# Seven block products in place of eight for the input product of a hybrid encoder layer, with its results passed through DRAM

## The chip, the cores and the metric

The kernel runs on one NeuronCore of a Trainium2 chip, in one launch. The metric is the time of the launch on the device, in microseconds (us). The engines are named as in the profile: PE (TensorE, with PEld for its weight loads), DVE (VectorE), ACT (ScalarE), POOL (GpSimd) and SP (SyncE, which here only issues DMAs).

## The reference

One encoder layer for 1024 positions of width 1024, in float32. The input is normalised and multiplied by one wide matrix; three branches use slices of the result, each branch's output goes through its own matrix and a gate, the sum through an output matrix, and a gated feed-forward block follows.

```python
h = rmsnorm(x, g[0])
proj = h @ w_in[l]
(mq, mk, mv, mo, mi, mf, dq, dk, dv, rq, rk, rv, rg, gates) = split_in(proj)
qk = jax.nn.silu(causal_dwconv(jnp.concatenate([mq, mk], axis=-1), mlstm_conv[l]))
hm = mlstm(mq_c, mk_c, mv, mi + bias_i, mf + bias_f)        # 4 heads of 256, scan over chunks
hm = jax.nn.sigmoid(mo) * head_rms(hm)
hd = diff_attention(dq, dk, dv, lam)                        # 8 heads, two softmaxes each
hr = jax.nn.silu(rg) * head_rms(retention(rq, rk, rv))      # 4 heads of 256, scan over chunks
y = (gm * (hm @ w_mlstm_out) + gd * (hd @ w_diff_out) + gr * (hr @ w_ret_out)) @ w_out
x = x + rmsnorm(y, g[1])
f = (silu(a) * u) @ w_ffn_out                               # a, u = split(rmsnorm(x) @ w_ffn_in)
x = x + rmsnorm(f, g[3])
```

The input matrix has 14344 columns: 112 blocks of 128, and eight columns for the mLSTM's input and forget gates.

## The kernel before, in words

Every large product is made of float32 operands that are split in two parts, a rounded high part and a low part (`split_sbuf`, L95 to L97: ACT casts, DVE subtracts), and of three matmuls per pair of operands (`mm3`, L99 to L104: high by high, high by low, low by high). All matmuls of these products carry the lines 102 to 104; the tiles tell the products apart.

The normalised input is turned to lie with its features on the partitions (`transposed`, L230) and held as `hh` and `hl` for the whole first half of the kernel. The input product runs in blocks. A `proj_block` (L192) makes 128 columns of the result for all positions: the weights are the stationary operand, 512 positions stream, eight steps along the features, two halves. A `nat_block` (L199) makes 256 columns of v with the positions on the partitions: 128 positions are stationary and 256 columns stream. A block's two halves are two passes of 24 matmuls, each cut into two steps, so a step is 12 matmuls of 512 columns; a step of a `nat_block` is 24 matmuls of 256.

What a block makes stays in SBUF in large tiles (tag `T`, 33 of 4 KB per partition) until its core has used it; only the gates go to DRAM. The mLSTM's q and k pass through a convolution of four taps (`conv_evac`, L342): one DVE multiplication and three multiply-adds, then Silu on ACT.

`stream` (L159) turns the list of blocks into a sequence of dense steps, with weights loaded two blocks and split one block ahead. Three cores run one after another: `mlstm_core` (L480), `diff_core` (L611) and `ret_core` (L745). Each is a generator that states how much of its work has passed, and `weave` (at the end of `trunk`) puts dense steps between its parts: 2.0 steps per unit of the two scans, 184 steps for the 832 units of the differential core. A scan has 32 chunks of 128 positions (4 heads by 8), two units each. The differential core has 64 turns, a head and a block of 128 queries each; the blocks of a head go from the longest (1024 keys) to the shortest (128 keys). In a turn the attention weights of one block are transposed, the scores of the next are made (PE L631, DVE L633 adds the bias and takes the maximum, ACT L638 takes the exponential, DVE L647 joins the two softmaxes), and the values of the first are multiplied (L668). Within these bounds a scheduler orders the instructions of each engine when the kernel is built, the earlier ones in the program first where they are ready.

Behind the cores come the branch products (`merge_blocks`, L823: 16 passes of two steps per branch, the gate's sigmoid and the sum of the branches on ACT and DVE), the output product (`out_blocks`) and the feed-forward block. The two products of the feed-forward block already use a scheme of seven products on a two by two grid of blocks: seven left operands (A11, A12, A22 and the sums S1 to S4, class `Seven`) by seven right ones (B11, B21, B22 and T1 to T4, class `Up`, L1025), 84 matmuls per pair of column blocks where the plain product has 96. Its start (`feed_forward`, L1129) works on two units while the left sums are made.

Of the kernel before, what the change touches and what calls it, by code (L numbers as in the profile page):

```python
# [36 lines left out]
N_T, N_WS, N_WH, N_WL, N_D, N_H = 33, 2, 4, 4, 4, 11  # L37
# [3 lines left out]
def trunk(ctx: ExitStack, tc: tile.TileContext, x, norm_gains, w_in, mlstm_conv, mlstm_gate_bias,  # L41
# [42 lines left out]
    g_dram = [dram.tile([D, S], F32, name=f"gate{i}") for i in range(3)]  # L84
    x2_dram = dram.tile([S, D], F32, name="x2_dram")
# [5 lines left out]
    def half_tile(shape=(P, HALF), dtype=F32):  # L91
        return small(list(shape), "s2k", dtype, bufs=N_H)
# [36 lines left out]
    class Block:  # L129
        def __init__(self, specs, run, own=False, pre=None):  # L130
            self.specs, self.run, self.own, self.pre = specs, run, own, pre
            self.stage = self.w = None

        def load(self):
            if self.stage is None:
                self.stage = []
                for src, shape in self.specs:
                    t = big(shape, F32, "ws") if self.own else pool.tile(shape, F32, tag="ws", bufs=N_WS, name=nm("ws"))
                    for a, part in src if isinstance(src, list) else [(src, t)]:
                        nc.sync.dma_start(part if part is t else t[:, :, part], a)  # L140
                    self.stage.append(t)
                if self.pre is not None:
                    self.pre()

        def split(self):
            self.load()
            if self.w is None:
                self.w = []
                for t, (_, shape) in zip(self.stage, self.specs):
                    if self.own:  # L150
                        hi, lo = big(shape, F32R, "wh"), big(shape, F32R, "wl")
                    else:
                        hi = pool.tile(shape, F32R, tag="wh", bufs=N_WH, name=nm("wh"))
                        lo = pool.tile(shape, F32R, tag="wl", bufs=N_WL, name=nm("wl"))
                    split_sbuf(hi, lo, t)
                    self.w.append((hi, lo))
# [26 lines left out]
    def proj_half(act, w, sh, evac):  # L183
        ps = psum(True)
        for kt in range(KT):
            mm3(ps, (w[0][:, kt, :], w[1][:, kt, :]), act.slot(sh, kt), kt == 0, kt == KT - 1)
# [4 lines left out]

    def proj_block(act, w_src, c, evac, order=(0, 1), **kw):  # L192

        def run(w):
            for sh in order:
                yield from proj_half(act, w[0], sh, evac)
        return Block([cols_of(w_src, c)], run, **kw)

    def nat_block(act, c, evac):  # L199

        def run(w):
            for st in range(NT):
                ps = psum(True)
                for kt in range(KT):
                    wh, wl = w[kt // 4]
                    mm3(ps[:, :256], act.tile(kt, st), (wh[:, kt % 4, :], wl[:, kt % 4, :]), kt == 0, kt == KT - 1)
                evac(ps[:, :256], st)
                yield
        return Block([cols_of(w_in, c, 256, k0, 4) for k0 in (0, 4)], run)
# [20 lines left out]
    def transposed(act, src, sh, g, wide=False):  # L230


        for kt in range(KT):
            ps = psum(wide and kt % 2 == 1)
            for i in range(4):
                nc.tensor.transpose(ps[:, i * P:(i + 1) * P], src[i][:, kt * P:(kt + 1) * P], ident)
            h, l = act.slot(sh, kt)
            nc.scalar.activation(h, ps, AF.Copy, scale=pcol[:, g + kt:g + kt + 1])
            yield nc.vector.scalar_tensor_tensor(l, ps, pcol[:, g + kt:g + kt + 1], h.bitcast(F32), op0=ALU.mult, op1=ALU.subtract)  # L239

    hT = Act("h")
# [9 lines left out]

    def gate_rows():
# [5 lines left out]
        lam_in = small([P, 4, 64], "s2k", bufs=N_H)  # L258
        nc.scalar.dma_start(lam_in, diff_lambda.broadcast_to([P, 4, 64]))
        lam_pr = small([P, 2, 64], "s2k", bufs=N_H)  # L260
# [34 lines left out]
        rows = big([P, S], name="rows")  # L295
        nc.vector.memset(rows, 0.0)
# [3 lines left out]
        reset = big([MH, S], name="reset")  # L300
# [650 lines left out]

# [506 lines left out]
```

## Time and profile before

| | us |
|---|---|
| median of 3 runs (lowest to highest) | 2686.84 (2686.42 to 2688.12) |
| the profiled execution, its own time | 2687.46 |
| its span in the profile | 2685.7 |
| PE busy / DVE / ACT / POOL | 2624.1 / 1403.5 / 1089.1 / 161.7 |
| mean granted clock of PE, share of full speed | 0.991 |

In the span mLSTM's chunks run from about 120 to 564 us, the differential core from 563 to 1258 us, the retention from 1260 to 1701 us; after that the rest of the branch products, the output product from about 1900 us, the feed-forward block from 2008 us with its down product from 2460 us. A row of a group gives line, engine, operation, tiles, count, busy time and mean duration; a row of a window gives the busy time of PE, PEld, DVE, ACT and POOL with the number of instructions in brackets, then PE's granted clock, the share of the DMA engines and GB/s. Matmuls of neighbours overlap in the profile, so distances between starts, or a window that PE fills, tell more than durations.

### The profile page before, as it was taken

How to read it: one execution, taken by the hardware profiler on the slowest of the kernel's cores; microseconds unless marked ns; L12 is line 12 of the kernel's file. 1: busy time of each engine (PE TensorE's matmuls, PEld its weight loads, DVE VectorE, ACT ScalarE, POOL GpSimd, SP SyncE). 2: the span in 40 equal slices, each digit the busy share in tenths (PEclk: the TensorE clock that was granted, in tenths of full speed). 3: DMA queues.
4: the chain of work that ended last, by engine and by line, in shares of the span. 5: the costliest groups of instructions: out<-in, count | busy, mean ns of one | idle time of the engine just before them, and what ended most of it. 6: DMA issues, size and time to landing. Idle time of an engine off the chain costs nothing.

```text
span 2685.7 us, 35232 instructions
## 1 busy us (share of the span) xinstructions
PE 2624.1 (98%) x13653; PEld 2212.7 (82%) x13653; DVE 1403.5 (52%) x2953; ACT 1089.1 (41%) x2119; POOL 161.7 (6%) x209
## 2 busy tenths in 40 slices
PE   7999999999999999999999999999989999998998
PEld 6889989888888888888889897888867888886886
DVE  5465564545554555544333335445477555555857
ACT  5644443334444444445333344422344333333444
POOL 0000000000000000000000000000020101110000
PEclk9999999999999999999999999999999999998999
DMA  4111112322222222211111234722431323338343
GB/s 146 48 56 56 56 56 64 95 75 81 54 79 60 75 79 60 79 40 52 47 44 37 63 102 134 226 88 71 157 133 63 102 87 106 106 104 297 113 124 107
DMA packets 244419, 243.08 MB, mean 91 GB/s; under 512 B 11838, under 2 KB 184335, under 8 KB 244251
## 3 DMA queue, kind: packets, MB, share of 16 engines
q1 hardware_dynamic: 242816, 238.63, 28.8%
q10 hardware_dynamic: 1434, 2.20, 0.3%
q8 instruction: 107, 1.75, 0.3%
q14 instruction: 62, 0.50, 0.1%
HBM read 178.62 MB, written 53.77 MB: 87 GB/s over the span
## 4 chain that ended last, share of the span: by engine, by line
PE 78%; issue 14%; DVE 3%; DMA 2%; POOL 1%; ACT 1%; SPq 0%; ACTq 0%; DVEq 0%; POOLq 0%
PE ps L103 23%; PE ps L104 23%; PE ps L102 23%; PE ps L631 2%; PE ps L668 2%; PE ps L657 1%; PE ps L461 1%; DVE wl L97 1%; DMA hid_S<-s2k 1%; PE ps L469 1%; POOL xr L216 0%; PE ps L429 0%; DMA s2k<-branch 0%; PE ps L686 0%; POOL s2k L1125 0%
## 5 line engine op out<-in xcount | busy, mean ns | idle before, releaser
L102 PE MATMUL ps<-hh,wh 128*128 128x512 f32 x1408 | 572.3, 406 | 1.9 <-DVE hl L239 1.9
L103 PE MATMUL ps<-hl,wh 128*128 128x512 f32 x1408 | 557.6, 396 | 0.0
L104 PE MATMUL ps<-hh,wl 128*128 128x512 f32 x1408 | 557.5, 396 | 0.0
L96 ACT CAST wh<-ws 128x1024 fp32r<-128x1024 f32 (+1 forms) x197 | 196.1, 999 | 431.1 <-PE ps L103 366.7
L97 DVE TENSOR_TENSOR wl<-ws,wh 128x1024 fp32r<-128x1024 f32 (+2 forms) x197 | 227.6, 1158 | 243.6 <-ACT wh L96 238.9
L104 PEld LDWEIGHTS ps<-hh,wl 128*128 128x128 f32 x1408 | 265.0, 188 | 63.1
L102 PEld LDWEIGHTS ps<-hh,wh 128*128 128x128 f32 x1408 | 265.8, 189 | 55.7 <-DVE hl L239 2.3
L103 PEld LDWEIGHTS ps<-hl,wh 128*128 128x128 f32 x1408 | 265.7, 189 | 53.5
L102 PE MATMUL ps<-wh,hh 128*128 128x256 f32 (+1 forms) x768 | 220.1, 287 | 0.0
L103 PE MATMUL ps<-wl,hh 128*128 128x256 f32 (+1 forms) x768 | 216.3, 282 | 0.0
L104 PE MATMUL ps<-wh,hl 128*128 128x256 f32 (+1 forms) x768 | 216.1, 281 | 0.0
L102 PE MATMUL ps<-bh,wh 128*128 128x512 f32 x384 | 153.0, 398 | 1.5 <-ACT bh L96 1.5
L103 PE MATMUL ps<-bl,wh 128*128 128x512 f32 x384 | 151.7, 396 | 0.3 <-DVE bl L97 0.3
L104 PE MATMUL ps<-bh,wl 128*128 128x512 f32 x384 | 151.6, 395 | 0.0
L102 PEld LDWEIGHTS ps<-wh,hh 128*128 128x128 f32 x768 | 145.0, 189 | 0.2
L103 PEld LDWEIGHTS ps<-wl,hh 128*128 128x128 f32 x768 | 145.0, 189 | 0.2
L104 PEld LDWEIGHTS ps<-wh,hl 128*128 128x128 f32 x768 | 144.9, 189 | 0.0
L102 PE MATMUL ps<-wh 128*128 128x512 f32 x308 | 120.4, 393 | 10.7 <-ACT wh L96 10.7
L103 PE MATMUL ps<-wl,wh 128*128 128x512 f32 x308 | 121.2, 393 | 1.8 <-DVE xv L215 1.1
L104 PE MATMUL ps<-wh,wl 128*128 128x512 f32 x308 | 120.8, 392 | 0.0
L638 ACT ACTIVATE sb<-sb,nmx 128x896 f32<-128x896 f32 (+7 forms) x128 | 98.6, 771 | 50.3 <-DVE nmx L637 49.7
L96 ACT CAST wh<-s2k 128x512 fp32r<-128x512 f32 x77 | 47.7, 620 | 113.1 <-PE ps L104 103.4
(300 smaller groups left out, 4994.1 us busy)
## 6 DMA issues: line engine op xcount, KB each, us to landing
ws<-in_w_in_dram SPq DMA_DIRECT2D x110, 512.0 KB, 4.1
ws<-in_w_ffn_in_dram SPq DMA_DIRECT2D x44, 512.0 KB, 3.9
gate<-s2k SPq DMA_DIRECT2D x48, 256.0 KB, 2.0
gl<-gate SPq DMA_DIRECT2D x24, 512.0 KB, 6.2
s2k<-branch SPq DMA_DIRECT2D x48, 256.0 KB, 5.9
hid_S<-s2k SPq DMA_DIRECT2D x44, 256.0 KB, 2.9
wd<-in_w_ffn_out_dram SPq DMA_DIRECT2D x22, 512.0 KB, 7.3
s2k<-hid_S SPq DMA_DIRECT2D x44, 256.0 KB, 2.6
```

The lines of the kernel that those rows point to most:

```text
L96: nc.scalar.copy(hi, src)
L97: nc.vector.tensor_sub(lo, src, hi.bitcast(F32))
L102: nc.tensor.matmul(ps, lh, rh, start=start, stop=False, skip_group_check=more)
L103: nc.tensor.matmul(ps, lh, rl, start=False, stop=False, skip_group_check=more)
L104: nc.tensor.matmul(ps, ll, rh, start=False, stop=stop, skip_group_check=more)
L461: nc.tensor.matmul(ps[:, :P], k_t[c // 4][:, j, half_cols(c)], q_t[c // 4][:, j, half_cols(c)], start=j == 0, stop=j == 1)
L469: nc.tensor.transpose(ps[:, j * P:(j + 1) * P], hn[:, j * P:(j + 1) * P], ident)
L631: nc.tensor.matmul(ps[:, :b - a], d["q", qb // 4][:, c, half_cols(qb)], d["k", n][i][:, c, :b - a], start=i == 0, stop=i == 1)
L638: nc.scalar.activation(sb[c], sb[c], AF.Exp, bias=nmx, scale=slope, accum_out=sm[:, c:c + 1])
L657: nc.tensor.transpose(ps[:, i * P:(i + 1) * P], u["sb"][0][:, kb * P:(kb + 1) * P], ident)
L668: nc.tensor.matmul(o_ps[:, :P], u["at"][kb // 4][:, half_cols(kb)], v[kb // 4][:, kb % 4, vc], start=kb == 0, stop=kb == qb)
```

## The change

All 112 column blocks of the input product are paired into 56 units, and each unit is made by seven products of 12 matmuls (class `Unit`, shared with the feed-forward block). The rows of the left operand are the two halves of the positions, its columns the two halves of the features; the sums S1 to S4 are made once (`left_sums`), the four differences of weights for each unit on DVE (on POOL for the three units at either start). The eight gate columns get products of their own (`gate_products`). v is made like everything else with its features on the partitions and is turned where it is needed.

Nothing a unit makes stays in SBUF: q, k, gate and v of the two scans go to `m_dram` and `r_dram`, q and k of the differential core in two parts to `qk_dram`, its v, turned, to `dv_dram`, the gates with their sigmoid applied to `g_dram`. A scan loads a chunk's eight rows of 128 positions one chunk ahead (`chunk_of`), the differential core loads a head's tiles while the head before runs (`diff_load`).

The order changes: mLSTM, then retention, both with 2.6 dense steps per unit; then the rest of the input product alone; then the differential core with 64 dense steps, which are now the products of the mLSTM and the retention branch; then the third branch. The sum over the branches passes through `y_dram`, the additions on POOL. The numbers of tiles change with it.

```diff
-N_T, N_WS, N_WH, N_WL, N_D, N_H = 33, 2, 4, 4, 4, 11
+N_T, N_WS, N_W, N_D, N_H = 32, 4, 5, 4, 14
...
+    y_dram = dram.tile([D, S], F32, name="y_dram")
+    m_dram = dram.tile([MH, P, 8, S], F32, name="m_dram")
+    r_dram = dram.tile([MH, P, 8, S], F32, name="r_dram")
+    qk_dram = dram.tile([DH, 2, 2, P, S], F32, name="qk_dram")
+    dv_dram = dram.tile([S, D], F32, name="dv_dram")
...
+        for role, dst, op, x, y in (("S1", "A22", ALU.add, "A21", "A22"), ("S2", "A22", ALU.subtract, "A22", "A11"),
+                                    ("S3", "A21", ALU.subtract, "A11", "A21"), ("S4", "A12", ALU.subtract, "A12", "A22")):
+            for i in range(2):
+                nc.vector.tensor_tensor(xs[dst, i], xs[x, i], xs[y, i], op=op)
+            for i in range(2):
...
+            (b11, b21), (b12, b22) = ((t[:, LO, :], t[:, HI, :]) for t in self.raw)
+            sub = {"T1": (b12, b12, b11), "T2": (b12, b22, b12), "T3": (b11, b12, b11), "T4": (b12, b21, b12)}
+            for r in roles:
+                if r in sub:
+                    src = sub[r][0]
+                    self.eng.tensor_tensor(*sub[r], op=ALU.subtract)
+                else:
+                    src = {"B11": b11, "B21": b21, "B22": b22}[r]
+                self.w[r] = parts_tile([P, 4, P])
+                split_sbuf(*self.w[r], src)
+        def product(self, ps, right, left, more):
+            wh, wl = self.w.pop(right)
+            for q in range(4):
+                mm3(ps, (wh[:, q, :], wl[:, q, :]), self.seven.slot(left, q), q == 0 and not more, q == 3, more)
...
+        def p6(self):
+            self.product(self.x, "T2", "S2", True)
+            self.b = self.kept(self.x)
...
+    def follow(u, after):
+        u.p1()
+        u.split("T3")
+        yield
+        u.p2()
+        u.split("B22")
+        yield
+        if after is not None:
+            after.load(0)
+            after.load(1)
+        u.p6()
+        u.split("T4")
+        yield
+        u.p5()
+        if after is not None:
+            after.split("B11")
+        yield
+        u.p7()
+        if after is not None:
+            after.split("B21")
+        yield
+        u.p3()
+        if after is not None:
+            after.split("T1")
+        yield
+        u.p4()
+        if after is not None:
+            after.split("T2")
+        yield
...
+        a, b, c = units
+        for u in units:
+            u.eng = nc.gpsimd
+        a.p1()
+        a.p2(False)
+        b.load(0)
+        b.load(1)
+        b.split("B11", "B21")
+        for _ in range(3):
...
+        sums = left_sums(seven, xs)
+        for u in units:
+            u.split("T1")
+        next(sums)
+        for u in units:
+            u.p5(False)
+            u.split("T2")
...
+        def evac(j, sh, ps, part):
+            if part is None:
+                part = half_tile()
+                nc.scalar.activation(part, ps, func or AF.Copy)
+            else:
+                nc.vector.tensor_add(part, ps, part)
+                if func is not None:
+                    nc.scalar.activation(part, part, func)
+            nc.sync.dma_start(dst(j)[:, halfs(sh)], part)
...
+            for i, t in enumerate((h, l)):
+                nc.sync.dma_start(qk_dram[hd, 1 - j, i][:, halfs(sh)], t.bitcast(F32))
...
+            for role, k in terms:
+                for q in range(4):
+                    w = wif[:, (k + q) * 16:(k + q) * 16 + P]
+                    for i, part in enumerate(hT.slot(role, q)):
+                        nc.tensor.matmul(ps, w, part, start=k == 0 and q == 0 and i == 0, stop=k > 0 and q == 3 and i == 1)
...
+    def chunk_of(src, u):
+        t = u["ch"] = big([P, 8, P], name="ch")
+        c = u["c"]
+        nc.sync.dma_start(t, src[u["hd"]][:, :, c * P:(c + 1) * P])
...
+    def natural_v(ch, ones):
+        ps = natural(ch, 6)
...
+        nc.sync.dma_start(spill[hd * HD:(hd + 1) * HD, c * P:(c + 1) * P].rearrange("(j p) s -> p j s", p=P), t)
...
+    def diff_load(hd, sh, d):
+        d["q", sh] = big([P, 2, HALF], F32R, "dq")
+        d["k", sh] = [big([P, 2, HALF], F32R, "dk") for _ in range(2)]
+        for i in range(2):
+            q, k = (qk_dram[hd, j, i][:, halfs(sh)].rearrange("(c p) s -> p c s", c=2) for j in range(2))
+            for a in range(2):
+                nc.sync.dma_start(d["k", sh][i][64 * a:64 * a + 64].bitcast(F32), k)
+            nc.sync.dma_start(d["q", sh][64 * i:64 * i + 64].bitcast(F32), q)
...
+        def half(o, sh, w):
+            rows = slice(o * P, (o + 1) * P)
+            g, y = half_tile(), None
+            nc.sync.dma_start(g, g_dram[b][rows, halfs(sh)])
+            if n > 0:
+                y = half_tile()
+                nc.sync.dma_start(y, y_dram[rows, halfs(sh)])
+            def evac(ps, sh):
+                nc.vector.tensor_mul(g, ps, g)
+                if n > 0:
+                    nc.gpsimd.tensor_tensor(g, g, y, op=ALU.add)
+                if n < 2:
+                    nc.sync.dma_start(y_dram[rows, halfs(sh)], g)
                 else:
-                    nc.vector.tensor_add(y[o][:, cs], y[o][:, cs], t[:, cs])
-                if b == 2:
                     h, l = yT.slot(sh, o)
...
+    hT, hx = Seven(), {}
+    def of(cols, evac, own=False):
+        return Unit(hT, w_in, cols, evac, own)
...
+        q, k, o, v = head(m_dram, (C_MQ, C_MK, C_MO, C_MV),
+                          (lambda dst, hd: convolved(dst, 2 * hd), lambda dst, hd: convolved(dst, 8 + 2 * hd),
+                           lambda dst, hd: stored(dst, AF.Sigmoid), lambda dst, hd: stored(dst)), hd)
+        units += [v, o, q, k]
...
+    for b in BRANCHES:
+        for o in range(0, KT, 2):
+            c = C_G + b * D + o * P
+            units.append(of((c, c + P), stored(lambda j, b=b, o=o: g_dram[b][(o + j) * P:(o + j + 1) * P, :], AF.Sigmoid)))
+    ups = [up(i, own=i == 2) for i in range(FB)]
+    units[2].own = True
...
+    def projections():
+        n = 7 * (len(units) - 3)
+        side = load_branch(BRANCHES[0], 0)
+        for i, _ in enumerate(steady(units[3:])):
+            made[0] = 3 + (i + 1) // 7
+            if i >= n - 4:
+                next(side, None)
+            if i == n - 3:
+                merges[0].load()
+            if i == n - 1:
+                for r in ROLES:
+                    hT.drop(r)
+                merges[0].split()
+            yield
...
+    def everything():
+        yield from projections()
+        yield from stream(merges + more)
...
+    begin(units[:3], hT, hx, turned(hn[4:], 1, 72, hT, hx))
...
-    weave(mlstm_core(), 2.0)
-    weave(diff_core(), 184 / 832)
-    weave(ret_core(), 2.0)
+    weave(mlstm_core(), 2.6)
+    weave(ret_core(), 2.6)
+    need(len(units))
+    weave(diff_core(), 64 / 832)
     for _ in dense:
         pass
-    feed_forward(ups, turns)
+    begin(ups[:3], h2, h2x, turns)
```

The bodies not shown: `turned` makes the high part, the plain float32 copy and the low part of three of the four quarters of the input (one ACT and two DVE operations per block); `convolved` is the convolution of before on tiles of half the width; `steady` runs `follow` over the units; `begin` goes on through all seven products, unit by unit for each; `keep_hidden` and the down product are as before but for the tiles of split weights, now of 512 columns each.

## Rows read from the trace of the kernel before

**Rows 1.** The page, part 1: busy time, share and instructions of each engine.

```profile
PE 2624.1 (98%) x13653; PEld 2212.7 (82%) x13653; DVE 1403.5 (52%) x2953; ACT 1089.1 (41%) x2119; POOL 161.7 (6%) x209
```

**Rows 2.** Windows of the span; stretch, length, each engine busy, clock, DMA, GB/s.

```profile
0.00:21.00 21.00, 7.34 (x34) 6.08 (x35) 8.52 (x19) 12.98 (x21) 2.51 (x9) 0.91 0.86 285
120.00:560.00 440.00, 438.73 (x2601) 385.47 (x2600) 243.36 (x645) 188.39 (x395) 20.03 (x31) 1.00 0.22 62
570.00:1250.00 680.00, 678.02 (x3812) 579.26 (x3811) 346.55 (x1005) 292.79 (x680) 33.97 (x62) 1.00 0.24 65
1260.00:1700.00 440.00, 437.56 (x2504) 379.12 (x2503) 174.11 (x368) 169.76 (x357) 17.53 (x32) 1.00 0.26 78
2000.00:2020.00 20.00, 11.29 (x48) 8.47 (x48) 14.73 (x21) 12.27 (x19) 2.80 (x3) 0.74 0.25 86
2100.00:2300.00 200.00, 200.00 (x859) 160.84 (x858) 107.84 (x133) 67.17 (x91) 30.45 (x23) 1.00 0.32 106
```

**Rows 3.** Waits of PE: who ended them, microseconds in total, times, longest.

```profile
PE ps L102 <- ACT wh L96: 15.1, 2, 10.7
PE ps L103 <- DVE S1l L97: 3.6, 1, 3.6
```

**Rows 4.** Timeline of PE: transposes; first and last of 85 matmuls.

```profile
32.70 0.60 PE L236 MATMUL ps<-ident,x 128*128 128x128 f32 x4
33.05 0.48 PE L102 MATMUL ps<-hh,wh 128*128 128x512 f32 x1
...
49.47 0.28 PE L104 MATMUL ps<-wh,hl 128*128 128x264 f32 x1
...
59.62 0.28 PE L104 MATMUL ps<-wh,hl 128*128 128x264 f32 x1
```

**Rows 5.** Groups by line over the whole span, the two input-product forms.

```profile
L102 PE MATMUL ps<-hh,wh 128*128 128x512 f32 x1408 | 572.3, 406 | 1.9 <-DVE hl L239 1.9
L102 PE MATMUL ps<-wh,hh 128*128 128x256 f32 (+1 forms) x768 | 220.1, 287 | 0.0
```

**Rows 6.** Groups by line over the span: DVE and ACT operations.

```profile
L97 DVE TENSOR_TENSOR wl<-wd,wh 128x512 fp32r<-128x512 f32 x77 | 52.7, 685 | 0.0
...
L352 DVE SCALAR_TENSOR_TENSOR q<-raw,pcol,q 128x512 f32<-128x512 f32 (+3 forms) x48 | 35.9, 748 | 0.7
L659 ACT COPY s2k<-ps 128x512 f32<-128x512 f32 (+1 forms) x64 | 32.3, 505 | 50.8 <-PE ps L657 50.3
```

**Rows 7.** Timeline of DVE and POOL, 2101.8 to 2106.3 us.

```profile
2101.82 1.70 POOL L1125 TENSOR_TENSOR s2k<-s2k,s2k 128x512 f32<-128x512 f32 x1
...
2102.28 1.78 DVE L1044 TENSOR_TENSOR t<-ws 128x512 f32<-128x512 f32 x1
...
2104.59 0.68 DVE L1045 TENSOR_TENSOR t<-t,ws 128x512 f32<-128x512 f32 x1
...
2105.19 1.21 DVE L97 TENSOR_TENSOR wl<-ws,wh 128x1024 fp32r<-128x1024 f32 x1
```

**Rows 8.** Groups by line, 120 to 560 us, then 570 to 1250 us.

```profile
L102 PE MATMUL ps<-hh,wh 128*128 128x512 f32 x385 | 156.2, 406 | 0.0
L102 PE MATMUL ps<-wh,hh 128*128 128x256 f32 x256 | 73.4, 287 | 0.0
...
L102 PE MATMUL ps<-hh,wh 128*128 128x512 f32 x597 | 243.1, 407 | 0.0
L102 PE MATMUL ps<-wh,hh 128*128 128x256 f32 x242 | 69.4, 287 | 0.0
```

**Rows 9.** Tiles dq and sb: score matmuls, then transposes; first and last start.

```profile
L631 PE MATMUL ps<-dk,dq x384: 220/389/505, 563.5 to 1249.3; 128*128 128x512 f32 x96, 128*128 128x384 f32 x32, 128*128 128x256 f32 x32, 128*128 128x128 f32 x32
...
L657 PE MATMUL ps<-ident,sb x288: 270/273/328, 570.8 to 1252.9; 128*128 128x128 f32 x144
```

**Rows 10.** DMA view: packets and bytes of the span, and weight loads.

```profile
DMA packets 244419, 243.08 MB, mean 91 GB/s; under 512 B 11838, under 2 KB 184335, under 8 KB 244251
...
ws<-in_w_in_dram SPq DMA_DIRECT2D x110, 512.0 KB, 4.1
```

More of the change, by code (lines that the diff above doesn't have):

```diff
@@ new lines, in steady @@
+    def steady(units):
+        chain = list(units) + [None]
+        for i in range(2):
+            chain[0].load(i)
+        chain[0].split("B11", "B21", "T1", "T2")
+        for u, after in zip(chain, chain[1:]):
+            yield from follow(u, after)
+    def follow(u, after):
[26 more added lines that the diff above has]
+            after.split("T2")
+        yield
@@ L856, in run, with two, one @@
+            return proj_half(bT[b], w, sh, evac)
+        def two(w, o, sides):
+            for sh in range(2):
+                steps = (s for j in range(2) for s in half(o + j, sh, w[j]))
+                yield from beside(steps, sides[sh], 1)
+        def one(o):
             def run(w):
-                steps = (s for sh in range(2) for s in proj_half(bT[b], w[0], sh, evac(o)))
-                side = load_branch(b + 1, 0) if b < 2 and o == KT - 2 else iter(())
-                yield from beside(steps, side, 2)
@@ L865, in merge_blocks @@
+        out += [Block([cols(o)], one(o)) for o in range(2, KT - 2)]
+        side = load_branch(BRANCHES[n + 1], 0) if n < 2 else nothing
+        out.append(Block([cols(KT - 2), cols(KT - 1)], lambda w: two(w, KT - 2, (nothing, side))))
         return out
@@ L1332, in trunk, with head @@
-    gb[-1].run = lambda w: beside(last_gate(w), first_branch, 2)
-    for b in range(3):
-        blocks += merge_blocks(b)
-    ups = [Up(i, own=i == 1) for i in range(FB)]
-    more, turns = out_blocks()
-    blocks += more
-    dense = stream(blocks)
-    def need(d):
-        while not d.get("ready"):
-            next(dense)
+    hT, hx = Seven(), {}
+    def of(cols, evac, own=False):
+        return Unit(hT, w_in, cols, evac, own)
+    def head(dst, cols, kinds, hd):
+        for i, (c, evac) in enumerate(zip(cols, kinds)):
+            c += hd * HD
+            yield of((c, c + P), evac(lambda j, i=i: dst[hd][:, 2 * i + j, :], hd))
@@ L1345, in trunk, with need @@
+    def need(n):
+        while made[0] < n:
+            next(dense)
+    merges = [b for n in range(3) for b in merge_blocks(n)]
+    more, turns = out_blocks()
+    def everything():
+        yield from projections()
+        yield from stream(merges + more)
+    dense = everything()
     nc.scalar.dma_start(ident, c_ident)
@@ L1359, in trunk @@
     load_x(4)
-    blocks[0].load()
+    units[0].load(0)
+    units[0].load(1)
     nc.scalar.activation(expo[:, 1:2], expo[:, 0:1], AF.Silu)
-    prow = small([P, P], "s2k", bufs=N_H)
+    prow = half_tile([P, P])
     nc.vector.memset(prow, 0.0)
```

825 lines of the change are left out of this document (338 added, 487 removed).

## Prediction

> **What bounds the kernel now.** I read the page's busy times first: PE is busy for 98% of the span, DVE for 52%, ACT for 41%, POOL for 6% [rows 1]. A busy PE need not be a PE at its peak, so the windows come next: from 120 to 1700 us PE hardly pauses and holds the full clock, beside all three cores alike; DVE is there at 40 to 55%, ACT at 39 to 43% [rows 2]. PE pauses only at the edges, while the first inputs arrive (7.3 of 21 us busy) and where the feed-forward block starts (11.3 of 20 us, at a granted clock of 0.74) [rows 2]; the wait view adds one of 10.7 us for a weight cast [rows 3], which is where the down product begins. So PE's matmul time sets the end, and a change is worth what it takes from PE less the pauses it opens.
>
> **The price of a matmul.** In a stretch where PE is never idle, 859 matmuls of 512 columns take 200 us, 0.233 us each [rows 2]. The narrow ones of 264 columns start 84 spacings apart over 10.15 us, 0.121 us each [rows 4], so 0.117 at 256. The durations printed in the groups are longer because neighbours overlap; they are not used. One step of the dense stream is 12 matmuls, 2.80 us. Four transposes delay the next matmul by 0.35 us, 0.088 each [rows 4].
>
> **Input product.** Each of the three groups in either form appears 1408 and 768 times [rows 5]. Removed are 4224 wide matmuls (984 us) and 2304 narrow ones, 192 of them at 264 columns (270 us): 1254 us. Added are 56 units of seven products of 12 matmuls, 4704 at 0.233: 1096 us. **Minus 158 us** on the engine that sets the end. The narrow form was no worse per column, so its disappearance gives nothing more.
>
> **What comes with it on PE.** The eight gate columns get 32 matmuls of their own (7.5 us); v, now stored transposed, costs 128 transposes in the two cores and 64 where the differential values are stored, and the gates eight (200 x 0.088 = 17.5 us). **Plus 25 us.** Net PE: -133.
>
> **Do the other engines still hide?** DVE gets per unit four subtractions, seven low parts and three additions out of PSUM: 14 operations on 512 columns. One lasts 0.685 us [rows 6], but in a run of them the next starts 0.60 us later [rows 7], so a unit is 8.4 us against 19.6 us on PE. A unit of mLSTM q or k has four convolutions of four operations more, 0.748 us for most [rows 6], 0.60 to 0.66 apart by the same overlap: about 10 us more. ACT's seven casts and four copies at 0.5 us or a little over [rows 6] are about 6 us a unit: not the bound. Stage by stage:
>
> - *Start.* The transposed input needs two DVE operations for three quarters of its blocks where it needed one, then eight sums on 1024 columns and their low parts; the twelve weight subtractions go to POOL. DVE then has 24 operations on the blocks (15 us), 16 on 1024 columns at 1.2 us [rows 7] (19), 21 low parts (13), nine additions (5) and one unit's convolutions (10), 62 us, under PE's 3 x 19.6 + 64 x 0.088 = 64 us. Something will stick out: +12, bounds 0 and +30.
> - *mLSTM core.* Of the 440 us window PE gives 1155 x 0.233 + 768 x 0.117 = 359 to dense work [rows 8], which leaves 2.6 us a chunk. Of DVE's 243 us [rows 2] 24 convolutions and 33 weight splits of 1.2 us [rows 7] leave 4.3 us a chunk. The new first half holds eleven units, six with convolutions, and 15.7 chunks: PE 11 x 19.6 + 15.7 x 2.7 = 258 us, DVE 92 + 60 + 68 = 220 us, 85%. The nearest row is this window, with DVE at 55% and PE waiting 1.3 us: it excludes little. I take +12, bounds 0 and +45 (DVE running at only 73% there).
> - *Retention core.* No convolutions, DVE near 60%: +2, bounds 0 and +10.
> - *Differential core.* It had 184 dense steps beside it, now 64. Of 680 us 417 + 85 were dense [rows 2, 8], so its own PE work is 178 us for some 62.5 units, 2.8 each. The new stage is 64 x 2.84 + 63 x 2.80 = 358 us if PE never waits. DVE: 346 us busy [rows 2] less 44 weight splits at 1.2 us and 56 operations on the q and k of seven heads at 0.685, 91 us, is 4.0 us a unit; with some 86 operations for two branches (52 us) 311 us, 87%. The latency counts as much: the first unit took 7.3 us from its first score matmul to its first transpose, the last, on 128 keys, 3.6 us from its last score matmul [rows 9]. The mean, about 5.4 us, has to fit into a turn of the loop of 358/64 = 5.6 us; it does on average, but a small block's turn is only 2 us of PE work and must borrow dense work from its neighbours. I take +25; the bounds are 0 and, with nothing overlapped, +135 (below).
> - *Between stages.* The input's parts hold 28 of 32 large tiles until the last unit, so the branch's and the heads' tiles are loaded only then; a weight tile of 512 KB takes 4.1 us to land [rows 10]. Some filling of the pipeline stays bare, and the last branch waits for the last head: +6, bounds 0 and +20.
> - *Feed-forward.* Three units instead of two share the start, so nine products stand ahead where PE now waits 3.6 us for a low part and 4.4 of the 15.1 us for a cast [rows 3]: -4, bounds -12 and +12 (the same DVE sums, and subtractions on POOL). The separate tiles for weight sums go, which frees large tiles for the down weights before the last up product ends; of the 10.7 us wait I take 7 off, bounds -11 and 0.
> - *DRAM.* Some 130 MB more beside 243 MB [rows 10], about 145 GB/s on average where 285 GB/s were moved in the first window [rows 2]; the chunks come in 512-byte runs as the input weights do, which land in 4.1 us. They are loaded one chunk, some 17 us, ahead on SP's queue, where the unit's two weight loads and four to eight stores now stand too: a store that waits there for its evacuation holds the loads queued behind it, and with them the next unit's first split, for which three products (8.4 us) are left. +0: what is late by less is covered by them.
>
> **Sum.** The profiled execution took 2687.5 us for a span of 2685.7; the median of the runs is 2686.8, so nothing needs scaling. 2687.5 - 133.5 + 12 + 12 + 2 + 25 + 6 - 4 - 7 = **2600 us**.
>
> **A rule that speaks against it.** Twelve subtractions at either start and 16 additions of the second and 16 of the third branch go to POOL. A DVE subtraction of two SBUF tiles took 1.78 us beside a POOL one of 1.70 us [rows 7], against 0.685 alone [rows 6]: each such meeting costs DVE 1.1 us. The Trainium skill, GPSIMD Engine Reference, section 1 (Specifications), says that POOL shares its SBUF interfaces with VectorE and contends with DVE instructions that have two SBUF inputs; the trace agrees, 1.78 against 0.685 us. By that rule the low parts, sums and subtractions all suffer, and the time would be the third rival's.
>
> **The rivals.**
>
> 1. *Everything stays hidden* (0.25). The scheduler fills gaps with later dense work, as in the three windows, where PE lost 1.3 to 2.4 us [rows 2]. Then +4, +3, 0, +10, +3, -8, -10: 2556 us. Against it: DVE at 85%.
> 2. *The differential loop runs bare* (0.10). If the dense steps are used up early, or the scores of the next unit find no free PSUM bank, a unit costs its chain of 5.4 us, then 1.8 us of transposes and value products and a copy of 0.5 us [rows 6]: 7.7 x 64 = 493 instead of 358, +135, and 2710 us with the other terms. It turns slower once a unit takes over 7.4 us, (358 + 113)/64, where 113 is what the other terms leave of the gain. Against it: before, PE almost never waited there, though with three times the dense work.
> 3. *DVE and POOL share a port and become the bound* (0.15) at both starts, with the convolutions and in the second half of the differential core: 24 + 16 meetings at 1.1 us are 44 us, and where DVE was at 85 to 97% nearly all of it shows: +15, +18, +17 on the forecast, 2650 us.
> 4. *The passage through DRAM shows* (0.05). If 1.4 us of a load stays bare at each of 64 chunks, 90 us of the gain go: 2690 us. Against it: the loads are a whole chunk ahead. The code does seven products, so that the change does nothing is not a case.
>
> **How the numbers follow.** The forecast has 0.45. Faster means under 2681.5 us (0.2%, about what a measurement can tell): the forecast, rivals 1 and 3, 0.85. Within 0.2%: most of rival 4, 0.04. Slower: rival 2 and the rest of 4, 0.11. The range runs from 2545, a little under rival 1, to 2695, past rivals 3 and 4; it leaves out rival 2 and the far ends, which need several bounds together.
>
> **What would show it.** Right: wide input matmuls 4224 to about 4704 with no narrow ones, at the same 0.233 us; PE 94 to 97% busy; the differential stage 360 to 400 us long with DVE above 75%; no 10.7 us wait for a cast. Wrong: PE waits on DVE low parts in the mLSTM stage of over 45 us, a differential stage over 430 us, waits for the chunk loads, or a granted clock under 0.95.

## The result, and the profile after

The changed kernel takes 2748.5 us (median of 4 runs, 2744.9 to 2750.2), the kernel before 2687.5 in the same comparison: a ratio of 1.0224, 95% interval 1.0207 to 1.0242. It is **slower by 2.2%**, where 2600 us was forecast, and outside the range. The profiled execution took 2744.9 us for a span of 2743.1. First the page, part 1, then windows of the changed kernel by stage, with columns as in [rows 2].

```profile
PE 2563.2 (93%) x12061; PEld 2083.4 (76%) x12061; DVE 1755.2 (64%) x3638; ACT 1222.5 (45%) x2480; POOL 262.5 (10%) x393
```

```profile
0.00:162.00 162.00, 127.24 (x518) 98.18 (x518) 118.66 (x187) 85.93 (x133) 27.68 (x36) 0.93 0.34 102
162.00:709.00 547.00, 544.22 (x2685) 451.21 (x2686) 404.83 (x917) 275.27 (x561) 27.71 (x148) 1.00 0.45 135
709.00:1286.00 577.00, 574.77 (x2878) 475.79 (x2877) 352.99 (x687) 275.79 (x560) 18.08 (x33) 1.00 0.49 141
1286.00:1381.00 95.00, 84.74 (x355) 66.83 (x354) 37.50 (x57) 35.60 (x61) 0.00 (x0) 0.95 0.59 160
1381.00:1857.00 476.00, 395.04 (x2051) 318.32 (x2052) 309.20 (x1021) 211.51 (x574) 58.62 (x80) 0.92 0.52 141
1857.00:2065.00 208.00, 197.78 (x852) 157.88 (x852) 107.74 (x157) 78.42 (x132) 42.54 (x36) 0.97 0.47 160
2065.00:2145.00 80.00, 72.27 (x288) 56.59 (x289) 63.05 (x73) 32.57 (x53) 26.57 (x14) 0.90 0.30 92
2145.00:2485.00 340.00, 340.00 (x1459) 273.95 (x1458) 199.77 (x277) 120.19 (x209) 49.96 (x36) 1.00 0.31 102
2485.00:2743.00 258.00, 227.18 (x985) 184.70 (x983) 161.45 (x266) 107.20 (x203) 11.32 (x12) 0.96 0.46 152
```

PE is busy for 61 us less than before [rows 1], though the span is 57 us longer: matmul work went, and pauses came. In order the windows are the start, the mLSTM core, the retention core, the rest of the input product, the differential stage, the third branch and the output product, the start of the feed-forward block, the rest of its first products, and the down product. PE is idle for 35 us in the first, for 2 to 3 in the next two, for 10, **81**, 10, 8, 0 and 31 in the others. In the differential stage the granted clock is 0.92 of full speed on average, and the fullest other engine, DVE, is busy for only 65%. The same three windows of the kernel before, at its start, its feed-forward block's start and its down product:

```profile
0.00:162.00 162.00, 147.03 (x773) 124.25 (x774) 94.13 (x190) 88.96 (x142) 7.33 (x15) 0.98 0.30 87
1975.00:2055.00 80.00, 64.63 (x274) 51.02 (x273) 63.41 (x81) 39.70 (x57) 5.88 (x8) 0.89 0.24 77
2420.00:2686.00 266.00, 241.64 (x1048) 197.85 (x1047) 169.21 (x275) 110.58 (x208) 11.22 (x12) 0.96 0.47 158
```

What PE waits for in the differential stage of the changed kernel (what it waited for, microseconds, times, longest):

```profile
PE ps L876 <- DVE sb L866: 38.5, 19, 6.8
PE ps L876 <- DVE dv L207: 24.6, 12, 2.8
```

L876 are the transposes of a unit's weights, L866 is the operation that combines its two score maps. (The second row is the same wait; `dv` was merely the later of two DVE operations to end.) One turn of the loop in the timeline of the changed kernel, from the transposes of a unit of 640 keys to those of the next, of 512:

```profile
1476.26 0.74 PE L876 MATMUL ps<-ident,sb 128*128 128x128 f32 x5
...
1476.75 1.36 PE L850 MATMUL ps<-dk,dq 128*128 128x512 f32 x4
...
1480.05 0.27 DVE L890 TENSOR_SCALAR ds<-ds,rec 128x1 f32<-128x1 f32 x1 [1.94 <-ACT junk L213]
...
1481.24 0.41 DVE L894 TENSOR_SCALAR hk<-ps,dfac,rec 128x128 f32<-128x128 f32 x1 [0.73 <-POOL dfac L208]
1481.57 0.68 DVE L852 CUSTOM_DVE_ANT_0 sb<-ps,ndist 128x512 f32<-128x512 f32 x1
...
1482.97 0.72 ACT L857 ACTIVATE sb<-sb,nmx 128x512 f32<-128x512 f32 x1 [0.66 <-DVE nmx L856]
...
1485.03 0.75 DVE L866 SCALAR_TENSOR_TENSOR sb<-sb,rat,sb 128x512 f32<-128x512 f32 x1
...
1485.93 0.63 PE L876 MATMUL ps<-ident,sb 128*128 128x128 f32 x4 [4.04 <-DVE sb L866]
```

The next unit's scores are done at 1478.1, yet DVE reads them at 1481.6: its queue holds the normalisation of the unit before (L890, L894) ahead of the reductions (L852: the sums with the bias, and their maxima). Then come two exponentials on ACT (the first is shown), the combination on DVE and at last the transposes, 9.7 us after the last ones. The turn before, in which nothing was blocked, took 6.6. The 64 units' transposes begin from 1388.7 to 1852.1, 463.4 us or 7.36 for each of the 63 turns; the stage's length in this sense is used below.

### The profile page after: what moved, and what is told of

Same layout as the page of the kernel before. It is cut to its first block, busy times and chain, and to the rows that moved or that the text cites. A ratio compares the mean times of both kernels' runs of the same rounds, so it can differ in the third digit from the quotient of the medians.

```text
span 2743.1 us, 35302 instructions
## 1 busy us (share of the span) xinstructions
PE 2563.2 (93%) x12061; PEld 2083.4 (76%) x12061; DVE 1755.2 (64%) x3638; ACT 1222.5 (45%) x2480; POOL 262.5 (10%) x393
## 5 line engine op out<-in xcount | busy, mean ns | idle before, releaser
L105 ACT CAST wh<-ws 128x512 fp32r<-128x512 f32 (+1 forms) x622 | 385.0, 623 | 748.2 <-PE ps L112 546.0
L106 DVE TENSOR_TENSOR wl<-ws,wh 128x512 fp32r<-128x512 f32 (+1 forms) x622 | 454.4, 734 | 234.3 <-ACT wh L105 228.9
L302 DVE TENSOR_TENSOR ws<-ws,ws 128x512 f32<-128x512 f32 x216 | 148.8, 689 | 99.8 <-DMA ws<-in_w_in_dram 56.1
L315 ACT COPY s2k<-ps 128x512 f32<-128x512 f32 x234 | 136.0, 582 | 17.8 <-PE ps L113 15.7
L111 PE MATMUL ps<-A11h,wh 128*128 128x512 f32 x312 | 127.8, 410 | 11.4 <-ACT wh L105 9.1
L111 PE MATMUL ps<-S1h,wh 128*128 128x512 f32 x312 | 127.1, 409 | 8.1 <-ACT S1h L105 7.5
L111 PE MATMUL ps<-S2h,wh 128*128 128x512 f32 x312 | 125.8, 404 | 3.6 <-ACT s2k L315 3.6
L111 PE MATMUL ps<-wh,wh 128*128 128x512 f32 x308 | 118.3, 392 | 11.4 <-ACT wh L105 11.4
L113 PE MATMUL ps<-A11h,wl 128*128 128x512 f32 x312 | 125.9, 403 | 2.3 <-DVE wl L106 2.3
L112 PE MATMUL ps<-S1l,wh 128*128 128x512 f32 x312 | 125.7, 403 | 1.5 <-DVE S1l L106 1.5
L112 PE MATMUL ps<-A11l,wh 128*128 128x512 f32 x312 | 125.6, 403 | 0.0
```

The source lines that it names most:

```text
L105: nc.scalar.copy(hi, src)
L106: nc.vector.tensor_sub(lo, src, hi.bitcast(F32))
L111: nc.tensor.matmul(ps, lh, rh, start=start, stop=False, skip_group_check=more)
L112: nc.tensor.matmul(ps, lh, rl, start=False, stop=False, skip_group_check=more)
L113: nc.tensor.matmul(ps, ll, rh, start=False, stop=stop, skip_group_check=more)
L302: self.eng.tensor_tensor(*sub[r], op=ALU.subtract)
```

## The experiments

Three theories were held against each other. **L**: the chain from one unit's transposes to the next unit's, with what it waits for in the engines' queues, takes over 7 us and stands bare, since only one dense step, 2.8 us, is left beside each unit. **D**: DVE is short of throughput, through the seven products' extra operations or because it meets POOL on one port. **M**: what passes through DRAM arrives late.

**Scores two units ahead** (a1). Each unit's chain then has two turns to run in.

```diff
         scores(units[0])
+        scores(units[1])
...
-            if after is not None:
-                scores(after)
+            if n + 2 < len(units):
+                scores(units[n + 2])
```

> The scores of a unit are issued two turns ahead instead of one; nothing else moves. Theory L (latency: the chain from one unit's transposes over the next unit's scores, reductions, exponentials and combination, 6.6 us at 640 keys, stands bare beside one dense step of 2.8 us): the chain has two turns to run in, the differential stage falls from 476 us to 380-410 (its matmuls need about 355), the granted clock there from 0.92 to 0.97 or more, the whole to 2650-2680. Theory D (DVE is short of throughput, through meetings with POOL on one port): the stage stays over 460 us and the whole at 2735-2755, for the same operations are issued. Theory M (the heads' loads from DRAM arrive late): the loads move one turn up, at most 10 us.

2664.4 us, ratio to before 0.9915 (0.9887 to 0.9944): 84 us gone by a change of order alone. The stage is 379.7 us (1386.6 to 1766.3). A window of it and its first waits:

```profile
1381.00:1767.00 386.00, 361.58 (x2020) 288.31 (x2019) 294.06 (x1007) 203.55 (x564) 57.98 (x77) 0.99 0.64 171
```

```profile
PE ps L850 <- DVE hk L894: 10.1, 19, 1.2
PE ps L876 <- DVE sb L866: 5.8, 6, 3.4
```

The same DVE operations fit into 90 us less, at 76% of DVE, and the wait for `sb` fell from 38.5 to 5.8 us, that for `dv` from 24.6 to 0.4: theory D is out for this stage, L holds. M is out as well: of the 10.2 us that PE waited for the heads' tiles in the changed kernel (the row stands under "Between stages" below), 9.5 fell ahead of the loop and 0.7 in it.

**No dense work beside the loop** (a2): `weave(diff_core(), 0)`.

> No dense step is woven into the differential loop; the two branches' products follow it whole. Theory L: what is left is the bare chain, about 6.2 us a unit, so the loop lasts some 400 us though its own matmuls are only 175; the 64 steps follow in 180 us, and the whole is 2745 + 400 + 180 - 476 = about 2850 (2810 to 2880). Theory D: the loop loses the branches' casts, products and POOL additions, 86 operations or 52 us of DVE and all meetings, and shrinks to 260-300 us; the whole is 2710-2750.

2909.6 us (+161). The loop, alone, lasts 455.9 us (1384.2 to 1840.1), only 7.5 less than with 64 dense steps in it:

```profile
1386.00:1840.00 454.00, 249.48 (x1292) 212.73 (x1291) 249.35 (x911) 171.45 (x502) 34.07 (x62) 0.78 0.28 64
```

PE and DVE are each busy for 55%, and still nothing is faster: this is the loop's chain with no dense work beside it, 7.2 us a turn. It is 56 us longer than I had expected from one unblocked turn of 640 keys, and queue order accounts for nearly all of that. In 14 of the 63 turns, all with units of 512 or 256 keys, the reductions begin directly behind the normalisation of the unit before:

```profile
1470.77 0.41 DVE L894 TENSOR_SCALAR hk<-ps,dfac,rec 128x128 f32<-128x128 f32 x1 [0.73 <-POOL dfac L208]
1471.09 0.68 DVE L852 CUSTOM_DVE_ANT_0 sb<-ps,ndist 128x512 f32<-128x512 f32 x1
```

Measured from a unit's first score matmul, they begin 3.0 to 5.7 us later there than in the quickest turn of the same length, 51 us in all. Without these the chain is 6.4 us a turn ((455.9 - 51) / 63).

**POOL's additions on DVE** (a3): in `merge_blocks`, `nc.vector.tensor_add(g, g, y)` in place of the addition on POOL.

> The 32 additions of the branch sums go from POOL to DVE. Theory D: 16 meetings in the second half of the differential stage at 1.1 us and 16 in the third branch vanish, 15 to 30 us come off, 2715-2730. Theory L: DVE has room (65% busy), but an addition of 0.69 us more may stand in its queue before the next unit's reductions: 2740-2765, the stage within 10 us of 476.

2754.1 us, the stage 473.2, ten more than without the edit. Taking POOL's additions away wins nothing here.

**Dense steps spread evenly** (a4):

```diff
-            w = (after["qb"] if after is not None else 0) + 3
+            w = 6.4
```

> The dense steps stand evenly, one after each unit, where they were weighted towards units with many keys. Theory L: a unit of many keys has the longest chain but also the most matmuls of its own, and loses cover; a unit of few keys gains it: -10 to +25 us, the waits for sb move from the head's last units to its first. Theory D: no change, 2735-2755.

2766.4 us (+18), the stage 483.8: within L's range, and the weighting towards units with many keys was the better one.

**The queue's order on DVE**, in two ways. First (b3) the normalisation was written behind the next unit's reductions, with a bank of the dense group for its input.

> On the changed kernel, scores one unit ahead as it has them: only the normalisation of a unit's output (four small operations on DVE and POOL) and its transposition move behind the next unit's score reductions, and the value products get a bank of the other group. If the queue order on DVE (the next unit's reductions stand behind the normalisation, which waits for ACT) is what makes the chain long: the stage 400-430 us instead of 474, the whole 2675-2705. If the bare chain alone is too long for one turn, whatever stands in DVE's queue: 455-475 us, the whole 2730-2750. Theory D: no change.

2767.1 us, the stage 479.9. The run decides nothing: in its timeline the normalisation (L897 there) still stands ahead of the reductions that it was written behind in 56 of 62 cases, for the order of a queue is not that of the source. So the operations were taken off DVE altogether (c1):

```diff
+            osb = half_tile([P, P])
+            nc.scalar.copy(osb, o_ps[:, :P])
-            nc.vector.tensor_scalar(ss, ss, r1, r1, op0=ALU.mult, op1=ALU.mult)
+            nc.gpsimd.tensor_scalar(ss, ss, r1, r1, op0=ALU.mult, op1=ALU.mult)
...
-            nc.vector.tensor_scalar(hn[:, :P], o_ps[:, :P], fac, r1, op0=ALU.mult, op1=ALU.mult)
+            nc.gpsimd.tensor_scalar(hn[:, :P], osb, fac, r1, op0=ALU.mult, op1=ALU.mult)
```

> On the changed kernel, scores one unit ahead as it has them: the normalisation of a unit's output leaves DVE; ACT copies the product out of PSUM (0.3 us) and POOL does the four small operations. DVE idled 37 us in the stage in front of L894, waiting for POOL's factor, while the next unit's score reductions stood behind it. If that blocking in the queue is what makes the chain too long, the stage falls from 474 to 430-445 us (the 37 us come off, no more) and the whole to 2700-2720. If the bare chain is too long without it, 465-480 us and 2735-2755. If POOL's longer chain now holds the output's transposition on PE, the stage grows: 480-500, 2750-2775.

2744.9 us, the stage 463.8 against 463.4. DVE's busy time falls by 38 us, and not a microsecond comes off. That looks as if the blocked turns cost nothing, but the timeline shows other work in the freed place. This is a turn of the same form as the blocked one above, a unit of 640 keys and then one of 512:

```profile
1710.61 0.71 PE L876 MATMUL ps<-ident,sb 128*128 128x128 f32 x5
...
1711.07 1.17 PE L850 MATMUL ps<-dk,dq 128*128 128x512 f32 x4
...
1715.60 0.62 ACT L105 CAST wh<-ws 128x512 fp32r<-128x512 f32 x1 [1.52 <-PE ps L112]
1716.25 0.69 DVE L106 TENSOR_TENSOR wl<-ws,wh 128x512 fp32r<-128x512 f32 x1 [4.55 <-ACT wh L105]
1716.86 0.68 DVE L852 CUSTOM_DVE_ANT_0 sb<-ps,ndist 128x512 f32<-128x512 f32 x1
...
1721.29 1.08 PE L876 MATMUL ps<-ident,sb 128*128 128x128 f32 x4 [5.49 <-DVE sb L866]
```

The scores are done at 1712.2. DVE then stands idle for 4.55 us, for the next operation in its queue is the low part of a dense step's weights (L106); that waits for its cast on ACT (L105), which itself waits for matmuls, and only then come the reductions. ACT has such turns as well: the copy that c1 adds, and casts, stand ahead of exponentials whose input is ready. The table counts reductions that begin over 1 us later after their unit's first score matmul than in the quickest turn of the same length, by what stands directly ahead of them, and exponentials that begin over 0.5 us after their input; in brackets the number of turns.

| | behind the normalisation | behind a dense step's low parts | exponentials late on ACT |
|---|---|---|---|
| changed kernel | 37 us (12) | 23 us (6) | 3 us (4) |
| c1 | 0 | 35 us (8) | 22 us (18) |

So c1 exchanged one wait in a queue for others of the same sum, about 60 us in both kernels, and does not show that queue order costs nothing. Without any such wait a long turn is still above the 5.6 us of PE work in a mean one: in c1 one from 896 to 768 keys took 7.5 us, with each part close behind the last:

```profile
1460.56 0.92 PE L876 MATMUL ps<-ident,sb 128*128 128x128 f32 x7
...
1468.02 0.84 PE L876 MATMUL ps<-ident,sb 128*128 128x128 f32 x6 [0.41 <-DVE sb L866]
```

No run has the loop with one unit's lead and both queues in the order that the chain wants; what that alone would give was not measured.

**More PE work for nothing** (e2). Six matmuls a unit were added, to separate the chain from the lower clock of a stage with pauses.

```diff
+            idle = psum(True)
+            for i in range(6):
+                nc.tensor.matmul(idle, diff_qk[hd]["q", qb // 4][:, i % 2, half_cols(qb)], diff_qk[hd]["k", 0][0][:, i % 2, :],
+                                 start=i == 0, stop=i == 5)
```

> On the changed kernel, scores one unit ahead as it has them: six more matmuls of 512 columns a unit, whose product nobody reads, 64 x 6 x 0.233 = 89 us of PE work at the full clock. If the chain alone sets the turn (theory L, the clock a consequence): the stage stays within 470-495 us and the whole within 2740-2765, for PE is idle 81 us of it. If the halved clock itself costs much (it stretches the scores, transposes and value products in the chain): the fillers raise the granted clock from 0.92 and the stage gets shorter, 440-465 us, 2710-2735. If PE's time set the stage: 476 + 89 = 565 us, 2835.

2748.7 us, against 2748.5 without: 89 us of matmuls cost nothing. The stage is 462.2 us; its window:

```profile
1386.00:1860.00 474.00, 456.97 (x2445) 368.87 (x2443) 306.90 (x1017) 211.85 (x574) 57.67 (x80) 1.00 0.52 140
```

PE is idle for 17 us and the clock is full, and the turn is as long as at 0.92 with 81 us idle. So the chain sets the turn, and the lower clock came of the pauses; no price of its own shows here.

**The kernel before, thinned and with the longer lead** (d1, d2). d1 writes `64 / 832` for `184 / 832` there; d2 is the edit of a1.

> On the kernel before, with nothing of the change in it: beside the same differential loop 64 dense steps are woven in place of 184; the other 120 run later. Theory L: the loop needs 7.1 us a unit however it is fed, so it lasts 455-480 us where its own work and 64 steps are about 358; the 120 steps cost their full time later, and the whole is 2687 + 100 to 120 = 2787-2807. Theory D or M (the seven products' DVE work, POOL, or the passage through DRAM make the changed kernel's stage slow): none of these is here, the loop lasts 360-390 us and the whole stays at 2687-2715.

> Control: the scores two units ahead in the kernel before. Theory L: three dense steps a unit, 8 us, already cover the chain there, so nothing is won: 2683-2691. If the older loop lost time to the chain as well, it gains 10 us or more.

d1 gave 2703.9 us (+18) and tells nothing of the theories: that loop pulls the input products of its own heads when it needs them, so that its stage stayed 642 us long with PE busy for 633 of them. Dense work was not thinned as meant. d2 gave 2681.6 us, ratio 0.9984 (0.9974 to 0.9995): 4 us, where the changed kernel won 84. In the kernel before the chain was indeed covered.

**The starts' subtractions on DVE** (b1, with a1): in `begin`, `u.eng = nc.vector`.

> On the version with the scores two ahead (2664): at both starts of seven products the twelve weight subtractions run on DVE instead of POOL. Theory D at the starts (DVE and POOL meet on one port: DVE's operations on 512 columns last 1.15 to 1.78 us there instead of 0.68): the meetings go, DVE's work from 20 to 120 us rises by 11 x 0.6 = 7 us and falls by 11 x 1.1 = 12 us, the starts together win 5 to 15 us: 2649-2659. Rival: the start is bound by the weights' landing and the order of the sums, so DVE's own time does not matter or the 7 us show: 2662-2672.

2644.4 us, 20 less than a1, from two runs that lie 9 us apart (2639.8 and 2649.0). DVE's groups from 20 to 120 us, of the changed kernel and then of b1:

```profile
L106 DVE TENSOR_TENSOR wl<-ws,wh 128x512 fp32r<-128x512 f32 x27 | 21.7, 822 | 4.9 <-ACT wh L105 4.9
L275 DVE TENSOR_TENSOR hx<-hx,hx 128x1024 f32<-128x1024 f32 x8 | 12.9, 1609 | 0.5 <-ACT hx L262 0.4
```

```profile
L106 DVE TENSOR_TENSOR wl<-ws,wh 128x512 fp32r<-128x512 f32 x27 | 17.9, 683 | 4.1 <-ACT wh L105 4.1
L275 DVE TENSOR_TENSOR hx<-hx,hx 128x1024 f32<-128x1024 f32 x8 | 9.8, 1219 | 0.4 <-ACT hx L262 0.4
```

Beside POOL's subtractions the same operations last 822 and 1609 ns on average, without them 683 and 1219. Theory D is supported at the starts, where DVE is busy for 81 of these 100 us, though not in the differential stage. The run does not separate it from a rival: POOL's subtractions themselves last 1.7 to 2.1 us there, the same ones on DVE 0.69, so the weights also come earlier. In the profiled executions 15 us came off, of which 8.6 lie ahead of the differential stage and 6.7 behind it.

**The down product's first loads ahead of the last stores** (b2, with a1): at the last but one step of `feed_forward` the four first blocks of `hid["A11"]` are loaded.

> On the version with the scores two ahead: the first four loads of hidden blocks for the down product are issued on SP's queue ahead of the last seven stores, four of which wait for POOL's sums. Theory Q (the 11.4 us wait of the first matmul of the down product for its cast is this order on SP's queue): the wait falls to 0-3 us and the whole by 8-14 us, to 2650-2657. Rival (the weights or the cast itself are late): the wait stays over 9 us, 2662-2666.

2652.9 us, 11.5 less than a1. The wait of PE at the down product, in the changed kernel and in b2:

```profile
PE ps L111 <- ACT wh L105: 11.4, 1, 11.4
```

```profile
PE ps L111 <- ACT wh L105: 0.5, 1, 0.5
```

The SP queue of the changed kernel shows the cause: four stores (x4) wait there for POOL's sums before the first load (L1230) is issued, and stores ahead of them had waited 10.5 us for DVE.

```profile
2501.94 4.62 SPq L1168 DMA_DIRECT2D hid_S<-s2k  x4
2506.61 3.29 SPq L1230 DMA_DIRECT2D s2k<-hid_A  x7
```

**Other banks for the loop's small products** (b4, with a1): `o_ps` and the output's transposition in `psum(True)`, score tiles of up to 512 columns in small SBUF tiles.

> On the version with the scores two ahead: value products and the output's transposition take PSUM banks of the dense group, and score tiles of up to 512 columns small SBUF tiles. What is left of waits there is 10 us of score matmuls for the read of a bank (L894) and 4 us of L904 for one: if those are banks, the stage falls from 380 to 362-372 us, the whole to 2648-2658; if they are DVE's own time, no change, 2660-2668.

2689.3 us, 25 worse than a1: the waits for a bank (L850 for L894) went, but L904 then waited 28.3 us for the same L894. The run suggests that the wait is for the normalisation's result and not for a bank; which of the three edits made it longer was not separated.

**Together.** c2 has a1, b1, b2 and four dense steps ahead of the first scores; e1 is c2 without those steps; e3 is e1 with c1's edit.

> The scores two units ahead, the weight subtractions of both starts on DVE, the first loads of the down product ahead of the last stores, and new here: four dense steps ahead of the differential stage's first scores, which cover their wait for the heads' loads from DRAM (8.7 to 13 us in the runs so far). If the four are independent: 2664 - 20 - 11.5 - 8 = about 2625 (2618 to 2635). If the four dense steps only move the wait: 2630-2640.

> The combined version without its four dense steps ahead of the differential stage: scores two ahead, weight subtractions of the starts on DVE, the down product's first loads ahead. If the four steps only moved the wait for the heads' loads: 2630-2643, no difference to the combined version's 2635-2644. If they gave the 8 us: 2643-2652.

> The three edits, and the normalisation of the differential output off DVE. With the scores two ahead PE still waited 10 us for the normalisation to free a bank and 4 us elsewhere in the loop: if DVE's queue order matters at this level, the stage falls from 380 to 365-372 us and the whole by 8-15 us against the three edits alone; if not, within 4 us of them.

c2: 2642.6 us (2635.8 to 2644.2). e1: **2635.9 us** (2633.1 to 2639.1), ratio to before **0.9812 (0.9798 to 0.9827)**, the best of all and faster than both kernels. The four steps gave nothing: the loop got 7 us shorter and began 9 later. e3: 2650.7 us, the stage 394.1 where e1 has 379.2: with two units' lead c1's edit costs 15 us, and PE now waits for POOL's result:

```profile
PE ps L908 <- POOL hk L898: 26.5, 31, 1.8
```

## Why the prediction was wrong

- **Differential core, +25 forecast, about +118 measured** (476 us for 358 of matmuls): the step that failed, two thirds of the error. It set a mean chain of 5.4 us against a turn of 5.6 and let it pass. That mean came from the first and the last unit alone, and it ended at the first transpose, though the next unit's scores stand behind all the transposes of this one. It also left no room for waits in DVE's queue. The runs show 7.2 us a turn with nothing beside it (a2), of which 6.4 are the chain itself and 0.8 waits in DVE's queue, and 7.36 with the dense step (1.76 more than 5.6: 63 x 1.76 = 111 us). Rival 2 had the bare loop, its price (7.7 us a turn) and the point from which it decides (7.4), at a chance of 0.10. What was held against it, that PE hardly waited there before, was the mistake: it spoke of a loop with three dense steps a unit (d2), and those were what the change took away. Of the rival's two causes, dense steps used up early and no free bank, neither was needed. The stage alone just uses up the gain, +118 against the 113 that the other terms were to leave; that the kernel is slower by as much as 61 us lies in the terms below.
- **DVE at 87% there**: it ran at 65% of a longer stage. Its operations were counted rightly (311 us forecast, 309 found); a busy share said nothing of a chain that passes through four engines in turn.
- **Input product, -158 + 25 on PE**: it came as far as counts tell. The groups of the changed kernel hold 6552 wide matmuls of the seven products, 1848 of them the feed-forward block's as before and 4704 the input product's, and no narrow ones. The price held too: from 2145 to 2485 us, where PE never pauses, 1459 matmuls of 512 columns take 340 us, 0.233 each.
- **Start, +12**: PE is idle for 35 us of the first 162 where it was for 15, and the clock is 0.93 for 0.98, together some 26 us by estimate: inside the bounds, near the upper one. 8.6 of it are the subtractions on POOL (b1), by their meetings with DVE or by their own length. The Trainium skill, GPSIMD Engine Reference, section 1 (Specifications), says that POOL's SBUF interfaces are shared with DVE; the trace agrees, 822 against 683 ns. Rival 3 had the starts right in kind, and the differential stage wrong (a3).
- **mLSTM and retention, +12 and +2**: 2 to 3 us of idle PE each. DVE at 74% hid everything. Too high by some 10.
- **Between stages, +6**: PE waited 9.5 us for the heads' loads from DRAM ahead of the first scores, and was idle for 10 us of that window and for 10 more between 1857 and 2065, with a clock of 0.95 and 0.97 that is worth another 10 by estimate: about +30, above the bounds. Rival 4, a wait at every chunk, did not happen. PE's waits for what had passed through DRAM, over the whole span, were for the heads' tiles and four times for a chunk of the mLSTM:

  ```profile
  PE ps L850 <- DMA dk<-qk_dram: 10.2, 2, 9.5
  PE ps L691 <- DMA ch<-m_dram: 5.4, 4, 2.6
  ```
- **Feed-forward start, -4**: right. PE is idle for 8 of 80 us, before 15.
- **Down, -7**: wrong. The wait is 11.4 us, where it was 10.7 [rows 3]. I took the weights to be late; it was the hidden blocks' loads, behind stores on SP's queue (b2), which the change did not touch. The whole stage has 31 us of idle PE where it had 24.

These terms (-133 + 26 + 4 + 118 + 30 - 8 + 6) make 2730 us of the 2745 that were profiled; 15 us were not located. Left open is how much of the differential stage's loss queue order alone would give back at one unit's lead: the late starts add up to about 60 us, but no run removes them all.

## What to carry to other kernels

When a change moves a loop beside less filler work, the loop's latency has to be priced anew: follow one turn from its first instruction back to itself, on several sizes, through every engine, and compare it with the PE work that will be left in a turn; that PE never waited there before says how much filler there was, not how short the chain is. Count the places where a part of the chain stands in a queue behind something that waits; and when an experiment takes the blocking operation away, look what stands there now before concluding that it cost nothing. If the chain is longer, a second unit in flight costs a few lines and two more score tiles, and here was worth 84 us, more than the change's own defect of 61. Look at what stands ahead of a stage's first loads on their queue too: loads that depend on nothing recent belong ahead of stores that wait.

## What had not been expected of the hardware

Matmuls can be free: with 89 us of them added, the time stayed at 2748.7 us and the granted clock rose from 0.92 to 1.00, so a stage that looks 96% full on PE (457 of 474 us) can still be bound by a chain; and no cost of the lower clock before showed either. Moving three small operations a unit from DVE to POOL changed nothing where the loop waited for its chain (c1), since waits behind other operations took their place, and cost 15 us with two units' lead (e3).
